# Low halves of the down projection's rest weights on VectorE, with two sums of product 6 moved behind them

## The chip, the cores and the metric

One core of a Trainium2 chip runs the whole program. The metric is the device time in microseconds. The kernel before takes 2112.26 us (median of 3 runs, 2108.97 to 2113.3). Engines are named as the profile names them: PE is TensorE's matmul and PEld its weight load, DVE is VectorE, ACT is ScalarE, POOL is GpSimd and SP is SyncE, which here only issues transfers. A line such as L361 is line 361 of the kernel before.

## The reference

Two layers of a decoder trunk on 512 tokens of width 1024, in float32. Each layer has a SwiGLU block, a mixer and a second SwiGLU block, each between two RMS norms:

```python
def swiglu(h, w_gate, w_up, w_down):
    return (jax.nn.silu(h @ w_gate) * (h @ w_up)) @ w_down

for l in range(DEPTH):                       # DEPTH = 2, D_MODEL = 1024, D_FF = 2816
    gn = norm_gains[l]
    h = rms_norm(x, gn[0])
    x = x + 0.5 * rms_norm(swiglu(h, w_ffn1_gate[l], w_ffn1_up[l], w_ffn1_down[l]), gn[1])
    ...
    x = x + rms_norm(mixed @ w_out[l], gn[3])
    h = rms_norm(x, gn[4])
    x = x + 0.5 * rms_norm(swiglu(h, w_ffn2_gate[l], w_ffn2_up[l], w_ffn2_down[l]), gn[5])
```

The change lies in the product with `w_down`, 2816 rows by 1024 columns, which runs four times: twice in each of two layers. Its result goes through a norm and is added to the residual x.

## The kernel before

**Precision.** Every float32 operand is split in two: a high half, rounded to the format that TensorE multiplies fast (`whi` for weights), and a low half, which is the operand less its high half (`wlo`). A product of two operands is three matmuls (`mm3`): high by high, high by low, low by high. In the down projection the activations are the stationary operand and the weights move, so the second of the three matmuls is the first one that reads `wlo`.

**The weight stream.** `ws` (class `Stream`) takes the weights in order through four raw buffers of 128x1024 (`w32`) and six pairs of split buffers (`whi`, `wlo`). An item is a raw weight or a combination of several. `ahead` splits items up to three ahead of the one in use, as long as fewer than six are in flight. A unit of kind "u" is split by a cast on ScalarE (L352) and a subtraction on VectorE (L361). A unit of kind "v" is split by the same cast, a multiplication by -1 on ScalarE that writes into the low half (L356), and a transfer issued by GpSimd that adds the raw weight to it (L359). When a raw buffer has been read, SP issues the load of a later weight into it.

**The down projection** (`down`, L698, with `fast` set in the four SwiGLU blocks). Its 22 blocks of 128 weight rows are treated in two ways. Blocks 0 to 15 with all columns and all tokens form a 2x2 matrix of quarters that is multiplied by seven products instead of eight (`quarters`, L927), in the order 1, 3, 7, 2, 6, 5 and, later, 4. Blocks 16 to 21 are the rest rows; they are multiplied directly, three units of two blocks for each half of the columns. The order on TensorE around the change is: product 6, product 5, the rest units' second column half for the token blocks 0 and 1, product 4, the same units for the token blocks 2 and 3, with transposes of the normed output between.

Each product has eight blocks in four pieces q = 0 to 3, one stream item each. A function of its own (`side1` to `side7`) is called before each piece, and brings the work that is to run beside it. The ones that matter here:

- `side6` splits activations for later products; at piece 3 it splits the first three of the six rest rows (`ready`, which casts on ScalarE at L430 and subtracts on VectorE at L431).
- `side5` splits the last three rest rows at piece 0. At piece 1 it issues the fetch (`fetch`): the output norm's gain and the eight tiles of the residual, 256 KB each, from memory (L737).
- `quarter` splits the pieces of the seven products (cast L285, subtraction L293) and forms the sums of weight quarters that later pieces need (L260).
- `add` (L943) sums product results into the output quarters on VectorE (L945). After product 6 come the sums into `c12` (from the first product's p1) and `u3`, after product 5 those into `c12` and `c22`. Each sum is two operations of 128x512, one for each token block.
- `half` (L830 to L833) adds the rest rows' result to the quarters' result, takes squares on ScalarE and multiplies by the gain. `post` (L851) adds it to the residual, `norm` (L862) prepares the next norm, and `turn` transposes the normed tokens for the next block on TensorE.

**Order.** TensorE's instructions run in the order of the text. Those of the other engines are ordered by the Tile framework's scheduler from the text's order and an estimate of times. `pin` ties an instruction behind the one that stands before it in the text on the same engine. `ws.hold` does so only while `ws.tight` is set, and casts of stream items are pinned while `ws.pinned` or `ws.tight` is set; `side6` sets `ws.pinned`. In the kernel before `ws.tight` is set only in the gate and up projections.

**Accumulators.** Five PSUM tiles are named `acc` and three `aux`. Products 6 and 5 write to two `acc` tiles each.

## Time and profile before

| | us |
|---|---|
| runs (3) | 2108.97, 2113.3, 2112.26 |
| median | 2112.26 |
| profiled execution, as timed | 2113.47 |
| its span on the profile | 2111.7 |
| mean granted clock of TensorE over the span | 0.989 |

The span runs from the program's first instruction to its last and is the basis of every view of the profile. Times in a timeline count from its start. A timeline row gives start and length, engine, line, operation, output and inputs by the program's names, the shape and how many like instructions are merged (x2), and in brackets the idle time of the engine just before, with what ended it. A row of waits gives who waited for whom, the microseconds in all, how many times, and the longest. Ends of matmuls are modelled: two in a row overlap on the page, so the pace of TensorE is read from their starts. A group row gives the count, the busy time in all and the mean of one in ns.

### The profile page before, as it was taken

How to read it: one execution, taken by the hardware profiler on the slowest of the kernel's cores; microseconds unless marked ns; L12 is line 12 of the kernel's file. 1: busy time of each engine (PE TensorE's matmuls, PEld its weight loads, DVE VectorE, ACT ScalarE, POOL GpSimd, SP SyncE). 2: the span in 40 equal slices, each digit the busy share in tenths (PEclk: the TensorE clock that was granted, in tenths of full speed). 3: DMA queues.
4: the chain of work that ended last, by engine and by line, in shares of the span. 5: the costliest groups of instructions: out<-in, count | busy, mean ns of one | idle time of the engine just before them, and what ended most of it. 6: DMA issues, size and time to landing. Idle time of an engine off the chain costs nothing. (4 is left out here: it accounts for less than half of the span.)

```text
span 2111.7 us, 36595 instructions
## 1 busy us (share of the span) xinstructions
PE 2083.1 (99%) x13561; PEld 1868.5 (88%) x13561; DVE 1621.3 (77%) x2897; ACT 1263.1 (60%) x2218; POOL 277.2 (13%) x330
## 2 busy tenths in 40 slices
PE   9999999999999999999999999999999999999997
PEld 7899987887888999998799998788778989999986
DVE  5887887766786787888788878967677758878886
ACT  6566686456454555658755666854654545666683
POOL 0011141000000011113101111400000000111140
PEclk9999999999999999999999999989999999999998
DMA  8677798312236368779858777973122553787794
GB/s 244 154 189 179 181 203 224 130 61 70 71 101 204 106 159 192 176 185 206 214 145 194 188 180 202 195 205 101 50 81 61 135 185 101 182 193 185 174 205 125
DMA packets 168531, 334.37 MB, mean 158 GB/s; under 512 B 19264, under 2 KB 85280, under 8 KB 168352
## 3 DMA queue, kind: packets, MB, share of 16 engines
q1 hardware_dynamic: 122416, 228.16, 32.4%
q0 software_dynamic: 45792, 103.83, 29.1%
q8 instruction: 106, 1.74, 0.3%
q14 instruction: 73, 0.60, 0.1%
q10 hardware_dynamic: 144, 0.05, 0.0%
HBM read 213.43 MB, written 14.73 MB: 108 GB/s over the span
## 5 line engine op out<-in xcount | busy, mean ns | idle before, releaser
L114 PE MATMUL acc<-s,whi 128*128 128x256 f32 (+1 forms) x4976 | 1051.3, 309 | 0.9 <-ACT whi L352 0.8
L114 PEld LDWEIGHTS acc<-s,whi 128*128 128x128 f32 x4976 | 808.8, 191 | 48.1 <-issue 3.2
L114 PE MATMUL acc<-s,wlo 128*128 128x256 f32 (+1 forms) x2488 | 764.8, 307 | 0.1
L114 PEld LDWEIGHTS acc<-s,wlo 128*128 128x128 f32 x2488 | 475.1, 191 | 23.1 <-DVE wlo L361 0.4
L114 PE MATMUL acc<-whi,s 128*128 128x512 f32 x1360 | 441.6, 393 | 0.0
L352 ACT CAST whi<-w 128x1024 fp32r<-128x1024 f32 (+1 forms) x309 | 287.0, 932 | 156.2 <-PE acc L114 89.8
L359 POOL DMA_DIRECT2D wlo<-w x190 | 163.6, 861 | 1292.1 <-DVE wlo L361 502.1
L352 ACT CAST whi<-tt 128x1024 fp32r<-128x1024 f32 x160 | 167.6, 1048 | 255.3 <-DVE tt L346 200.6
L114 PEld LDWEIGHTS acc<-whi,s 128*128 128x128 f32 x1360 | 255.3, 188 | 57.6 <-ACT whi L352 1.6
L361 DVE TENSOR_TENSOR wlo<-tt,whi 128x1024 fp32r<-128x1024 f32 x160 | 196.0, 1225 | 136.0 <-ACT whi L352 133.7
L114 PE MATMUL acc<-wlo,s 128*128 128x512 f32 x680 | 265.2, 390 | 0.2 <-DVE wlo L293 0.2
L114 PE MATMUL aux<-s,whi 128*128 128x256 f32 (+1 forms) x1296 | 239.2, 285 | 0.0
L361 DVE TENSOR_TENSOR wlo<-w,whi 128x1024 fp32r<-128x1024 f32 (+1 forms) x119 | 143.3, 1213 | 81.4 <-ACT whi L352 79.6
L114 PEld LDWEIGHTS aux<-s,whi 128*128 128x128 f32 x1296 | 202.7, 192 | 1.1 <-issue 0.5
L114 PE MATMUL aux<-s,wlo 128*128 128x256 f32 (+1 forms) x648 | 184.3, 284 | 0.0
L356 ACT ACTIVATE wlo<-w 128x1024 fp32r<-128x1024 f32 (+1 forms) x190 | 165.7, 873 | 0.0
L114 PE MATMUL aux<-whi,s 128*128 128x512 f32 x432 | 153.2, 414 | 0.0
L114 PEld LDWEIGHTS acc<-wlo,s 128*128 128x128 f32 x680 | 127.8, 188 | 25.6 <-DVE wlo L293 0.6
L442 POOL DMA_DIRECT2D s<-s x128 | 111.0, 958 | 220.6 <-ACT s L430 100.4
L114 PEld LDWEIGHTS aux<-s,wlo 128*128 128x128 f32 x648 | 124.4, 192 | 0.3
L293 DVE TENSOR_TENSOR wlo<-s,whi 128x512 fp32r<-128x512 f32 x160 | 102.6, 685 | 12.5 <-ACT whi L285 12.4
L114 PE MATMUL aux<-wlo,s 128*128 128x512 f32 x216 | 91.7, 425 | 19.5 <-DMA wlo<-w 19.5
(181 smaller groups left out, 2474.1 us busy)
## 6 DMA issues: line engine op xcount, KB each, us to landing
w<-wall SPq DMA_DIRECT2D x267, 512.0 KB, 4.2
wlo<-w POOLq DMA_DIRECT2D x110, 512.0 KB, 5.4
w<-wall SPq DMA_DIRECT2D x224, 128.0 KB, 3.6
wlo<-w POOLq DMA_DIRECT2D x80, 256.0 KB, 3.4
s<-wall SPq DMA_DIRECT2D x128, 128.0 KB, 3.9
s<-s POOLq DMA_DIRECT2D x64, 256.0 KB, 4.5
x_d<-s SPq DMA_DIRECT2D x48, 256.0 KB, 2.1
s<-x_d SPq DMA_DIRECT2D x48, 256.0 KB, 6.6
```

Source lines behind the costliest of these rows:

```text
L114: nc.tensor.matmul(o, lhsT, rhs, start=start, stop=stop)
L293: pin(nc.vector.tensor_tensor(it.lo[:, h[c]], w[c], it.hi[:, h[c]].bitcast(F32), op=ALU.subtract))
L352: i = nc.scalar.copy(it.hi[:, c], w[:, c])
L356: i = nc.scalar.mul(it.lo[:, c], w[:, c], -1.0)
L359: nc.gpsimd.dma_start(it.lo[:, c].bitcast(F32), w[:, c], accum_op=ALU.add)
L361: self.hold(nc.vector.tensor_tensor(it.lo[:, c], w[:, c], it.hi[:, c].bitcast(F32), op=ALU.subtract))
L442: nc.gpsimd.dma_start(lo.bitcast(F32), src, accum_op=ALU.add)
```

## The change

Three things change. The rest units of the second column half become kind "u". In `side5` the last three rest rows are split at piece 1 instead of piece 0, and `ws.tight` is set there; it stays set until product 5's last sum. And the sum of product 6 into `u3` is kept back (`late.then`) and made at piece 3 of product 5; `add` now goes through `ws.hold`, so while `ws.tight` is set the sums keep the place that the text gives them.

`ahead` comes to the first rest unit in piece 0 of product 5, to the second in piece 1, to the third in piece 2 and to product 4's first piece in piece 3. So the text's order on VectorE from there on is: first rest unit's low half, last three rest rows, second and third unit's low halves, the two sums into `u3`, product 4's first piece, the sums into `c12` and `c22`.

```diff
@@ rows
-            def unit(j, h, kind="u"):
+            def unit(j, h):
                 c = 2 * j * P
                 self.src[self.n] = ...
-                self.plain(1, kind)
+                self.plain(1)
...
             for j in lead:
-                unit(j, 1, "v" if fast else "u")
+                unit(j, 1)
@@ down
             def side5(q):
-                if q == 0:
+                if q == 1:
+                    ws.tight = True
                     ready(kt)
-                elif q == 1:
                     fetch()
+                elif q == 3:
+                    late.then()
@@ quarters
         def add(o, a, b):
             for t in range(2):
-                nc.vector.tensor_tensor(o[t], a[t], b[t], op=ALU.add)
+                ws.hold(nc.vector.tensor_tensor(o[t], a[t], b[t], op=ALU.add))
             return o
...
         c12 = add(p1, p, p1)
-        add(u3, p, u3)
+        late.then = lambda p=p: add(u3, p, u3)
         p = product(5, two(acc), True, side=side5)
         add(c12, p, c12)
         c22 = add(two(big), p, u3)
+        ws.tight = False
```

## The prediction

> **What bounds the kernel now.** I read the page first, then TensorE's own waits, then the stretch where they lie, engine by engine.

> ```profile
> span 2111.7 us, 36595 instructions
> ...
> PE 2083.1 (99%) x13561; PEld 1868.5 (88%) x13561; DVE 1621.3 (77%) x2897; ACT 1263.1 (60%) x2218; POOL 277.2 (13%) x330
> ```
> ```profile
> PE aux L114 <- DMA wlo<-w: 19.5, 12, 5.0
> ```

> The matmul stream is the kernel: PE is busy for all but 28.6 us. Of that idle time 19.5 us lie in twelve waits for the transfer that finishes a weight's low half (`wlo`). Twelve is three rest units in each of four down projections, so these are the instructions the change touches. The timeline of PE in the first of the four, and the windows of all four, show that the waits cost more than their own length:

> ```profile
> 322.81 0.39 PE L114 MATMUL aux<-whi,s 128*128 128x512 f32 x1
> 326.43 0.79 PE L114 MATMUL aux<-wlo,s 128*128 128x512 f32 x1 [3.23 <-DMA wlo<-w]
> ...
> 330.73 0.79 PE L114 MATMUL aux<-wlo,s 128*128 128x512 f32 x1 [1.37 <-DMA wlo<-w]
> ...
> 333.91 0.80 PE L114 MATMUL aux<-wlo,s 128*128 128x512 f32 x1 [0.26 <-DMA wlo<-w]
> ```
> ```profile
> 326.43:335.77 9.34, 7.71 (x16) 5.14 (x17) 2.10 (x4) 2.36 (x6) 0.00 (x0) 0.50 1.05 300
> ```
> ```profile
> 311.92:322.81 10.89, 10.89 (x49) 9.01 (x48) 10.89 (x19) 9.71 (x15) 2.73 (x4) 1.00 0.98 249
> 322.81:340.11 17.30, 12.44 (x37) 8.71 (x36) 9.48 (x17) 6.72 (x16) 0.86 (x1) 0.70 0.96 287
> 1019.43:1036.23 16.80, 12.68 (x37) 8.87 (x36) 9.47 (x17) 6.89 (x16) 0.86 (x1) 0.70 0.97 293
> 1366.38:1386.46 20.08, 13.77 (x37) 9.69 (x36) 10.16 (x18) 7.95 (x17) 1.15 (x2) 0.66 0.84 250
> 2065.79:2081.56 15.77, 11.60 (x37) 8.06 (x36) 9.52 (x18) 7.35 (x16) 0.86 (x1) 0.78 0.69 175
> 311.92:351.02 39.10, 34.24 (x134) 26.76 (x133) 27.92 (x54) 25.36 (x48) 4.45 (x6) 0.87 0.80 229
> ```

> A window's columns are its length, then busy time of PE, PEld, DVE, ACT and POOL, the granted clock, the share of DMA time and GB/s. The first of these six is product 5: 48 matmuls in 10.89 us, 0.2269 us each, at clock 1.00. The next four start at the first matmul of the rest units and end at the first one of product 4. Between them stand 36 matmuls (two token blocks, six rows, three products), 8.17 us at that pace. They take 17.30, 16.80, 20.08 and 15.77 us, so **the rest units lose 9.13 + 8.63 + 11.91 + 7.60 = 37.3 us**: 19.5 of waiting, and the rest because the clock stands at 0.50 once the first wait is over, for 9.34 us in the first projection.

> Why the low half is late:

> ```profile
> 316.73 1.05 ACT L352 CAST whi<-w 128x1024 fp32r<-128x1024 f32 x1 [1.08 <-issue]
> 317.69 1.05 ACT L356 ACTIVATE wlo<-w 128x1024 fp32r<-128x1024 f32 x1
> ...
> 320.85 1.06 ACT L352 CAST whi<-w 128x1024 fp32r<-128x1024 f32 x1
> ```
> ```profile
> 319.03 0.86 POOL L359 DMA_DIRECT2D wlo<-w  x1 [6.11 <-DMA w<-wall]
> ```
> ```profile
> s<-x_d SPq DMA_DIRECT2D x8, 256.0 KB, 8.3
> wlo<-w POOLq DMA_DIRECT2D x3, 512.0 KB, 9.6
> ```

> The first weight is cast at 316.73, its negative is made by 318.74, and the adding transfer is issued at 319.03. Between 318 and 327 these three transfers take 9.6 us (median) to land, among eight 256 KB reads of the residual (8.3 us). PE wants the first low half at 323.03 and gets it at 326.4.

> **The change, part by part.**

> *Low halves on VectorE.* Per projection three ScalarE multiplies, three POOL issues and three 512 KB transfers go; three 128x1024 subtractions on VectorE come.

> ```profile
> L361 DVE TENSOR_TENSOR wlo<-w,whi 128x1024 fp32r<-128x1024 f32 x117 | 142.1, 1222 | 81.4 <-ACT whi L352 79.6 <-DMA w<-wall 0.6 <-DMA grow<-rows_d 0.3
> ```

> That is 3 x 1.22 = 3.67 us more on VectorE and 3 x 1.05 us (row 317.69) less on ScalarE. VectorE is the engine to watch: in product 5 it is busy 10.89 us of 10.89. So I lay out its order as the program pins it. E is the moment after product 5's last weight piece is split, R the first matmul of the rest units.

> ```profile
> 319.44 1.28 DVE L945 TENSOR_TENSOR s<-acc,s 128x512 f32<-128x512 f32 x2
> 320.64 1.88 DVE L431 TENSOR_TENSOR s<-s,s 128x512 fp32r<-128x512 f32 x3
> ...
> 336.21 0.69 DVE L830 TENSOR_TENSOR s<-aux,s 128x512 f32<-128x512 f32 x1 [7.68 <-PE aux L114]
> ```
> ```profile
> 1015.82 1.28 DVE L945 TENSOR_TENSOR s<-acc,s 128x512 f32<-128x512 f32 x2
> ```
> ```profile
> 1363.59 1.28 DVE L945 TENSOR_TENSOR s<-acc,s 128x512 f32<-128x512 f32 x2
> ```
> ```profile
> 2062.25 1.27 DVE L945 TENSOR_TENSOR s<-acc,s 128x512 f32<-128x512 f32 x2
> ```

> These rows, the sums of product 6 that now move, start at E: 319.44, 1015.82, 1363.59, 2062.25. With R from the windows, R - E is 3.37, 3.61, 2.79 and 3.54 us. A 128x512 operation costs 0.60 in a row (319.44 to 320.64 for two). In the changed kernel the first subtraction stands at E (its cast, done at 317.8, comes before), so the first low half is there at E + 1.2; the last three rows' splits end at E + 3.0, the second low half at E + 4.2, the third at E + 5.4. The third cast, which started at 320.85 when it stood behind two multiplies, ends at 321.9 at the latest, before VectorE is ready for it at 323.6. PE needs the low halves at matmuls 1, 7 and 13: R + 0.23, R + 1.59, R + 2.95, which is E + 3.6, 4.96, 6.32 in the first projection and E + 3.0, 4.38, 5.74 in the third, the tightest. All three are in time, by 0.2 to 2 us. **The whole 37.3 us leave this stretch.**

> *The moved steps.* The last three rows' casts on ScalarE now stand behind the first weight's cast, which waits for its weight until 316.73; each has half its width, so some 0.5 us, and they end at about 319.4. VectorE takes them from E + 1.2 = 320.6, so its own work hides the move; without that cover it would cost the 1.6 us of the three casts. The nine transfers of the fetch stay in the same piece of product 5 on SP's queue. The loads of the next weights, which had waited for the adding transfers, can now go among them from E + 1.2 on; the residual they might push back is first read at L851, 17 us after E. The two sums of product 6 (1.2 us) go behind the third low half. They hold two accumulators until E + 6.6; with those of product 5 and one of y all five are taken, and the next is asked for after product 4, 19 us after R.

> *What is late next.* Behind the third low half VectorE has the two sums (to E + 6.6), product 4's first piece (two splits, two sums, to 9.0), four sums of product 5 (11.4), two products with the gain (12.6), one sum of the first token block (13.2), the second and third piece of product 4 (14.4, 15.6), then the chain that ends in the residual, L851, which starts at E + 17.6. The cover that hid all this before was the 7.68 us in which VectorE waited for PE (row 336.21), and it is gone: from the start of product 5 to the end of product 4 VectorE was busy 27.92 of 39.10 us and now has about 31.4 in 30.0. PE is at product 4 at R + 8.17 and needs its second piece at R + 11.12, which is E + 14.5 in the first projection (0.1 to spare) and E + 13.9 in the third (0.5 late). Further on I compare lags:

> ```profile
> 341.64 1.41 DVE L851 SCALAR_TENSOR_TENSOR s<-s,rt,s 128x512 f32<-128x512 f32 x2
> ...
> 350.50 0.89 DVE L862 TENSOR_SCALAR s<-s,rt 128x512 f32<-128x512 f32 x2
> ```
> ```profile
> 355.08 0.60 PE L124 MATMUL acc<-ident,s 128*128 128x128 f32 x4
> ```
> ```profile
> 2086.54 1.41 DVE L851 SCALAR_TENSOR_TENSOR s<-s,rt,s 128x512 f32<-128x512 f32 x2
> ```
> ```profile
> 2090.62 1.04 PE L124 MATMUL acc<-ident,s 128*128 128x128 f32 x8
> ```

> Before, L851 starts 1.5 us after product 4 does (341.64 against 340.11); afterwards E + 17.6 against E + 11.5, 6.1 after it: VectorE lags 4.5 us more. The transposes at 355.08 had 4.1 us to spare on their first operand (350.50 + 0.44), so they wait up to 0.4 us, and 0.6 more in the third projection, whose R - E is shorter. In the last, the transposes at 2090.62 had 3.4 us on theirs (2086.54 + 0.71): 1.0 late. I take 0.4, 0.3, 1.0 and 1.0, **about 3 us given back**. Bounds: nothing, if the pinned order lets the critical operations go first; 4 x 2.5 if every lag of 4.5 comes out 2 us longer.

> [...]

> **The sum.** 37.3 - 3 = 34.3 us off the profiled 2111.7. The profiled execution took 2113.47 in all, the runs 2108.97 to 2113.3 with median 2112.26, all within 0.2% of each other. From the median: **2078 us**. Its own range is 2074.5 (nothing given back) to 2084.

> **The rivals.**

> *A long wait stays in two projections.* For it: the third projection has 0.2 us to spare at the second low half, and PE already waited 0.20 there for product 5's last piece:

> ```profile
> 1363.73 0.50 PE L114 MATMUL acc<-wlo,s 128*128 128x512 f32 x1 [0.20 <-DVE wlo L293]
> ```

> [...] Price: two times about 9.3 back, 2097 us.

> *The half clock has another cause than the waits.* Then only the waiting goes: 19.5 - 3, so 2096 us. Against it: 1.00 stands right before and the four stretches alone are slow.

> *It does not do what it says.* The subtractions come out behind other work in VectorE's queue and the halves arrive when the transfers did: 2112 us. The pins speak against it.

> *VectorE becomes the bound, and it is slower.* One mechanism: the third low half is over 3 us late, for instance because its weight lands late. Everything pinned behind it, sums, product 4's pieces, norms, is then late by the same, and PE meets one short wait after another up to the transposes, which keep the clock at half as the waits at 330.73 and 333.91 did. From there to product 4's end are 5.2 + 10.9 = 16.1 us of work: 16.1 more, with 3 of waiting 19 a projection, against 9.3 now. In three projections of four that is 3 x 9.7 - 8.6 = 20 us slower, 2133. For it: 31.4 us of work in 30.0. Against it: it takes 4 us more than the layout has at the third low half.

> **Chances.** Forecast 0.68; long wait in two 0.13; half clock stays 0.05; no effect 0.04; VectorE bound 0.10. Faster by over 0.2% (4.2 us, about what this kernel's measurement can tell) holds the first three: 0.86; within it 0.03; slower 0.11. The range 2074 to 2098 takes in the forecast and the first two rivals but for their edges.

> **What would show it.** No wait of PE for `wlo<-w` in the aux matmuls and clock 1.00 between product 5 and product 4, 8.2 us long in each projection; VectorE's subtraction right after product 5's last split, and no 7.68 us idle before L830; new waits of PE under 1 us each at product 4's second or fourth piece or at the transposes. Wrong would be a wait over 3 us anywhere there, or a first subtraction that starts after R.

## Result and profile after

The changed kernel takes 2078.21 us (median of 5 runs, 2077.91 to 2081.02) against 2112.48 us before (5 runs, 2108.97 to 2116.1). The ratio is 0.984, with a 95% interval of 0.9825 to 0.9854: 34.3 us, 1.6%, faster. In what follows lines of the changed kernel are shifted by two or three: L947 is the old L945, L832 the old L830, L835 the old L833, L853 the old L851, L864 the old L862.

The page of the changed kernel, its span, busy times and granted clock by slice:

```profile
span 2076.3 us, 36563 instructions
...
PE 2067.7 (100%) x13561; PEld 1860.7 (90%) x13561; DVE 1632.1 (79%) x2909; ACT 1251.3 (60%) x2206; POOL 268.2 (13%) x318
...
PEclk9999999999999999999999999999999999999999
```

PE is idle for 8.6 us of the span instead of 28.6. VectorE has twelve more instructions, GpSimd and ScalarE twelve fewer each: three in each of four projections. Who PE still waits for, all rows of that view:

```profile
PE acc L124 <- DVE s L853: 3.1, 2, 2.6
PE aux L114 <- DVE eps_t L137: 1.1, 1, 1.1
PE acc L114 <- DVE s L531: 0.3, 1, 0.3
```

The twelve waits for `wlo<-w` are gone, with nothing in their place in the rest units. The windows of these units in the first two projections, from their first matmul to product 4's first:

```profile
323.04:331.20 8.16, 8.16 (x38) 6.76 (x36) 8.16 (x13) 3.99 (x10) 0.00 (x0) 1.00 1.03 392
1010.59:1018.81 8.22, 8.22 (x38) 6.81 (x37) 8.22 (x13) 4.16 (x10) 0.00 (x0) 1.00 1.01 374
```

They were 17.30 and 16.80 us at clock 0.70. The other two run from 1348.76 to 1356.92 and from 2036.59 to 2044.75, 8.16 us each. So the four gave up 9.14 + 8.58 + 11.92 + 7.61 = 37.3 us. VectorE's timeline in the first projection shows the layout:

```profile
319.46 1.22 DVE L361 TENSOR_TENSOR wlo<-w,whi 128x1024 fp32r<-128x1024 f32 x1
320.60 1.89 DVE L431 TENSOR_TENSOR s<-s,s 128x512 fp32r<-128x512 f32 x3
322.40 2.36 DVE L361 TENSOR_TENSOR wlo<-w,whi 128x1024 fp32r<-128x1024 f32 x2
324.67 1.29 DVE L947 TENSOR_TENSOR s<-acc,s 128x512 f32<-128x512 f32 x2
...
331.87 0.69 DVE L832 TENSOR_TENSOR s<-aux,s 128x512 f32<-128x512 f32 x1
...
336.88 1.41 DVE L853 SCALAR_TENSOR_TENSOR s<-s,rt,s 128x512 f32<-128x512 f32 x2
```

The first low half is made at 319.46, as soon as product 5's last piece is split, and the other two stand in a pair at 322.40, the third ready at 324.76. From product 5 to L853 no row has idle time in brackets any more: the 7.68 us before L832 are used up.

The rest of the account comes from laying the starts of all 13,561 matmuls of the two traces side by side. Each row gives by how much the changed kernel came out ahead (minus) or behind (plus) in a stretch:

| stretch | us |
|---|---|
| start-up of the program | +0.2 |
| rest units, four projections | -37.3 |
| projection 3, product 5's last piece no longer waited for | -0.5 |
| product 4's pieces, projections 1 to 4 | +0.07, +0.32, +0.35, +0.28 |
| last projection, transposes and what follows | +1.26 |
| sum, up to the last matmul | -35.3 (spans: 2076.3 - 2111.7 = -35.4) |

### The profile page after: what moved, and what is told of

Its sections match the earlier page's. It is cut to its first block, busy times and chain, and to the rows that moved or that the text cites. A ratio compares the mean times of both kernels' runs of the same rounds, so it can differ in the third digit from the quotient of the medians.

```text
span 2076.3 us, 36563 instructions
## 1 busy us (share of the span) xinstructions
PE 2067.7 (100%) x13561; PEld 1860.7 (90%) x13561; DVE 1632.1 (79%) x2909; ACT 1251.3 (60%) x2206; POOL 268.2 (13%) x318
## 4 chain that ended last, share of the span: by engine, by line
PE 95%; DVE 2%; DMA 1%; ACT 1%; issue 1%; SPq 0%; DVEq 0%; ACTq 0%
PE acc L114 72%; PE aux L114 21%; PE aux L124 2%; DMA w<-wall 1%; DVE wlo L293 1%; DVE s L260 1%; PE acc L124 0%; DMA s<-xin 0%; DMA s<-wall 0%; DVE s L947 0%; SPq L240 0%; DVE s L853 0%; SPq L243 0%; ACT s L440 0%; ACT s L530 0%
## 5 line engine op out<-in xcount | busy, mean ns | idle before, releaser
L114 PE MATMUL acc<-s,whi 128*128 128x256 f32 (+1 forms) x4976 | 1051.4, 309 | 0.3 <-DVE s L531 0.3
L114 PEld LDWEIGHTS acc<-s,whi 128*128 128x128 f32 x4976 | 808.8, 191 | 47.5 <-issue 3.2
L114 PE MATMUL acc<-s,wlo 128*128 128x256 f32 (+1 forms) x2488 | 764.8, 307 | 0.1
L114 PEld LDWEIGHTS acc<-s,wlo 128*128 128x128 f32 x2488 | 475.1, 191 | 23.1 <-DVE wlo L361 0.4
L114 PE MATMUL acc<-whi,s 128*128 128x512 f32 x1360 | 441.7, 393 | 0.0
L352 ACT CAST whi<-w 128x1024 fp32r<-128x1024 f32 (+1 forms) x309 | 287.0, 933 | 160.3 <-PE acc L114 93.7
L352 ACT CAST whi<-tt 128x1024 fp32r<-128x1024 f32 x160 | 167.7, 1048 | 256.1 <-DVE tt L346 199.8
L359 POOL DMA_DIRECT2D wlo<-w x178 | 154.3, 867 | 1258.6 <-DVE wlo L361 496.6
L114 PEld LDWEIGHTS acc<-whi,s 128*128 128x128 f32 x1360 | 255.3, 188 | 57.4 <-issue 1.6
L361 DVE TENSOR_TENSOR wlo<-tt,whi 128x1024 fp32r<-128x1024 f32 x160 | 196.1, 1225 | 137.2 <-ACT whi L352 133.7
L114 PE MATMUL acc<-wlo,s 128*128 128x512 f32 x680 | 265.5, 390 | 0.0
L114 PE MATMUL aux<-s,whi 128*128 128x256 f32 (+1 forms) x1296 | 239.2, 285 | 0.0
L361 DVE TENSOR_TENSOR wlo<-w,whi 128x1024 fp32r<-128x1024 f32 (+1 forms) x131 | 157.7, 1214 | 82.7 <-ACT whi L352 81.7
L114 PEld LDWEIGHTS aux<-s,whi 128*128 128x128 f32 x1296 | 202.7, 192 | 1.1 <-issue 0.5
L114 PE MATMUL aux<-s,wlo 128*128 128x256 f32 (+1 forms) x648 | 184.3, 284 | 0.0
L356 ACT ACTIVATE wlo<-w 128x1024 fp32r<-128x1024 f32 (+1 forms) x178 | 153.3, 861 | 0.1
L114 PEld LDWEIGHTS acc<-wlo,s 128*128 128x128 f32 x680 | 127.7, 188 | 26.5 <-DVE wlo L293 1.7
L114 PE MATMUL aux<-whi,s 128*128 128x512 f32 x432 | 143.6, 390 | 0.0
L114 PEld LDWEIGHTS aux<-s,wlo 128*128 128x128 f32 x648 | 124.4, 192 | 0.3
L293 DVE TENSOR_TENSOR wlo<-s,whi 128x512 fp32r<-128x512 f32 x160 | 102.8, 688 | 9.9 <-ACT whi L285 9.9
L430 ACT CAST s<-s 128x512 fp32r<-128x512 f32 (+1 forms) x140 | 70.6, 547 | 44.5 <-DVE s L489 41.0
## 6 DMA issues: line engine op xcount, KB each, us to landing
w<-wall SPq DMA_DIRECT2D x267, 512.0 KB, 4.1
wlo<-w POOLq DMA_DIRECT2D x98, 512.0 KB, 5.4
wlo<-w POOLq DMA_DIRECT2D x80, 256.0 KB, 3.4
s<-s POOLq DMA_DIRECT2D x64, 256.0 KB, 4.5
x_d<-s SPq DMA_DIRECT2D x48, 256.0 KB, 4.5
s<-x_d SPq DMA_DIRECT2D x48, 256.0 KB, 5.2
```

What stands on the lines that cost most here:

```text
L114: nc.tensor.matmul(o, lhsT, rhs, start=start, stop=stop)
L293: pin(nc.vector.tensor_tensor(it.lo[:, h[c]], w[c], it.hi[:, h[c]].bitcast(F32), op=ALU.subtract))
L352: i = nc.scalar.copy(it.hi[:, c], w[:, c])
L356: i = nc.scalar.mul(it.lo[:, c], w[:, c], -1.0)
L359: nc.gpsimd.dma_start(it.lo[:, c].bitcast(F32), w[:, c], accum_op=ALU.add)
L361: self.hold(nc.vector.tensor_tensor(it.lo[:, c], w[:, c], it.hi[:, c].bitcast(F32), op=ALU.subtract))
```

## Experiments

Each kernel was timed against runs of the kernel before on the same chip.

**The subtractions alone.** The kernel before with its order untouched and only the kind of the units changed:

```diff
-                unit(j, 1, "v" if fast else "u")
+                unit(j, 1)
```

> The kernel before with the rest units' low halves on VectorE, and nothing else: the last three rows and the sums of product 6 keep their old place ahead of the first subtraction. Theory (the late transfers were the loss; the order only trims what VectorE is late): the first low half ends at E + 1.2 + 1.8 + 1.2 = E + 4.2 and PE needs it at E + 3.6, 3.8, 3.0 and 3.8 in the four projections, so one wait of 0.4 to 1.2 us each, clock 1.00; 2 to 3 us more than the changed kernel: about 2080.5. Rival (without the new order VectorE is late enough to halve the clock): two or more projections lose some 9 us again, 2095 or more.

Measured: 2080.27 us (2079.89 to 2081.72), ratio 0.9846 (0.9831 to 0.986), span 2079.9. The waits in the rest units are now VectorE's own:

```profile
PE aux L114 <- DVE wlo L361: 3.1, 4, 1.1
```

So replacing the transfers gives all but about 2 us. What the order adds is visible as these four waits of 0.39 to 1.12 us; in the times alone it is near the limit of what they can tell.

**The order alone.** The changed kernel, with the low halves made by the transfers as before:

```diff
-                unit(j, 1)
+                unit(j, 1, "v" if fast else "u")
```

> The changed kernel's order and pins, with the low halves made as before, by ScalarE and an adding transfer. Theory (the transfers are the loss): PE still waits for them some 4 us or more in each projection and the clock falls to 0.50 behind it; 2108 to 2120. Rival (the order alone frees the path): 2080 to 2095.

Measured: 2108.84 us (2106.31 to 2112.04), ratio 0.998 (0.9971 to 0.999), span 2108.3.

```profile
PE aux L114 <- DMA wlo<-w: 19.8, 10, 3.9
```

The waits for the transfers are what they were before (19.5 us). The moved splits and sums do nothing about them. In the second projection, against the expectation, the clock did not fall behind its waits of 2.90, 0.81 and 1.35 us: it is 1.00 from 1021.21 to 1029.21. The time is still some 4 us under the kernel before. The mean granted clock of the two profiled executions is 0.994 here and 0.989 before, which goes the same way; whether the order or chance did that, no run shows.

**The sums of product 6 in their old place.** The changed kernel without the deferral:

```diff
-        late.then = lambda p=p: add(u3, p, u3)
+        add(u3, p, u3)
```

> The changed kernel with the two sums of product 6 back ahead of the rest units' low halves. Theory: every low half comes 1.2 us later than in the changed kernel, the second at E + 5.35 against a need of E + 4.4 to 5.2: waits of 0.2 to 1 us in each projection, clock 1.00, 1.5 to 2.5 us in all: about 2080. Rival (the moved sums carry the gain): over 2090.

Measured: 2079.49 us (2078.36 to 2080.34), ratio 0.9841 (0.9826 to 0.9855), span 2077.1. The two sums then stand before the second low half and PE waits 0.56 us in the first projection and 0.73 us in the second, 1.3 us in all; the other two show no wait, though one was expected in each. The span grows by 0.8 us. The direction is the expected one, but against the changed kernel's 2078.21 the times overlap.

**The residual's reads taken out of the transfers' way.** The kernel before, with the eight reads of the residual issued behind the loads of the next weights:

```diff
+            if not fast:
+                reads()
+        def reads():
...
-                    nc.sync.dma_start(xt[t][h], x_d[t, h])
+                    i = nc.sync.dma_start(xt[t][h], x_d[t, h])
+                    if fast:
+                        pin(i)
```

> The kernel before with the eight reads of the residual put behind the loads of the next weights on SP, so that the adding transfers have no such reads beside them. Theory (each transfer is late by crowding, and the clock falls only after a wait of some 3 us): the transfers land in about 5.4 us instead of 9.6, PE waits about 1.2 us at the first and 1 to 2 us at the second and third, and the clock stays at 1.00 where no wait is over 3 us; about 4 us a projection, 2090 to 2098 if the later reads hold up nothing else. Rival 1 (a transfer takes its 7 to 10 us without the reads too): no change, 2112. Rival 2 (any wait halves the clock): waits shorter, slow stretch as before, about 2103.

Measured: 2106.02 us (2103.54 to 2106.7), ratio 0.9964 (0.9951 to 0.9977), span 2101.8: a miss by 8 us or more. Ten waits of 18.5 us remain. The DMA issues with their median times to landing, first in the first projection (319 to 326 us), then in the last (2050 to 2060 us):

```profile
wlo<-w POOLq DMA_DIRECT2D x3, 512.0 KB, 5.3
w<-wall SPq DMA_DIRECT2D x1, 512.0 KB, 7.5
...
s<-x_d SPq DMA_DIRECT2D x8, 256.0 KB, 10.2
wlo<-w POOLq DMA_DIRECT2D x3, 512.0 KB, 9.8
```

The last projection has no weights left to load, so there the reads went out beside the transfers as before, and the transfers took 9.8 us; where the reads came later they took 5.3. So beside the reads the transfers took nearly twice as long here (in the kernel before, 9.6 us in the first projection). But without them the first transfer, issued at 320.16, still landed at 324.73, 4.6 us later and 1.7 us after PE asked for it, and the third, with the next weight's load beside it, took 7.9 us. PE's waits in the first projection:

```profile
324.77 0.50 PE L114 MATMUL aux<-wlo,s 128*128 128x512 f32 x1 [1.74 <-DMA wlo<-w]
327.59 0.51 PE L114 MATMUL aux<-wlo,s 128*128 128x512 f32 x1 [1.16 <-DMA wlo<-w]
332.10 0.50 PE L114 MATMUL aux<-wlo,s 128*128 128x512 f32 x1 [2.85 <-DMA wlo<-w]
```

PE asked for the first low half at 323.03, 2.9 us after the issue: the quickest of the three transfers took 4.6 us and could not meet that. Nor would 4.6 us have done from the issue in the kernel before, at 319.03, 4.0 us ahead. The three waits, 5.75 us in all, cost this projection little more than their length (6.6 us by the starts of the matmuls, against the changed kernel): the matmuls behind them take 0.50 us on the page, not the 0.79 of the kernel before, and the granted clock is 1.00 from 327.59 to 336.10. In the third projection it fell behind a wait of only 2.83 us (0.73 from 1364.18 to 1370.60). Both asked for the next set.

**A wait put back without any transfer.** The changed kernel, with n extra sums of 128x512 into an unused buffer (counted on at 0.60 us each) pinned on VectorE behind the first low half, so that the second and third come later. Nothing is left out of the computation.

```diff
                 if q == 1:
                     ws.tight = True
+                    idle = big()
+                    for _ in range(n):
+                        pin(nc.vector.tensor_tensor(idle, src[kt - 1], src[kt - 1], op=ALU.add))
                     ready(kt)
```

n = 4:

> The changed kernel with four extra 128x512 sums on VectorE (2.4 us, their result is not used) right behind the first rest unit's low half. The second low half is then about 1.4 us too late (it had about 1 us to spare). Theory (a short wait costs its own length, no clock with it): one wait of 1.2 to 2 us in each projection, clock 1.00; 6 to 10 us more than the changed kernel, 2084 to 2088. Rival (any wait halves the clock): 4.5 us more in each, 2102 or more. Rival (VectorE has slack all along): 2078 to 2080.

n = 6:

> The same with six extra sums (3.6 us; their result is not used): one wait of 2.5 to 3.2 us in each projection. Theory: just under or at the length after which the clock falls; 2089 to 2093 where it holds in all four, 4.5 us more for each projection where it falls, up to 2111. Rival (the low clock came with the transfers, not with the waiting): 2089 to 2093 and 1.00 in all four.

n = 8:

> The same with eight extra sums (4.8 us; their result is not used): one wait of 3.6 to 4.4 us in each projection. Theory (idle time halves the clock, whatever it waits for): clock 0.50 behind each wait for some us; 15 to 19 us of waiting and about 4.5 a projection for the clock, 2108 to 2116. Rival (the low clock came with the transfers): 1.00 behind the waits, 2093 to 2097.

n = 2, and n = 6 once more:

> Two extra sums of 0.60 us behind the first low half, so everything behind it is 1.2 us later. The four and the six extra sums left waits of 1.50 to 1.83 us for 2.4 us and 3.04 to 3.23 us for 3.6 us added, so 0.4 to 0.9 us of delay were hidden in each projection. If only what is not hidden counts, the waits here are 0.3 to 0.8 us each, with a few tenths behind them at product 4, the clock stays at 1.00 in all four stretches, and the time is 2080 to 2083 us. If short waits can cost the clock too, as the 1.82 us wait did with four sums, at least one stretch shows a clock under 0.8 and the time is 2083 to 2090 us.

> The kernel with six extra sums once more. In its first profile waits of 3.23, 3.04, 3.06 and 3.18 us left the clock at 1.00, 0.63, 1.00 and 0.63. If what decides lies in the program (which projection, what went before), the second and fourth projection are slow again and the span is within 1 us of 2097.9. If it lies in the moment, where a wait falls against something that runs on its own, other projections or another number of them are slow, and each one more or less moves the span by some 4 us.

| n | added as measured, four projections | median us (runs) | span over the changed kernel's | PE's waits for `wlo` in the rest units |
|---|---|---|---|---|
| 2 | 5.3 | 2086.59 (2086.52 to 2087.22) | +8.6 | 1.02, 0.23, 0.31, 0.46 |
| 4 | 11.1 | 2091.23 (2090.64 to 2091.79) | +12.6 | 1.83, 1.82, 1.71, 1.50 |
| 6 | 17.0 | 2100.15 (2098.53 to 2101.61) | +21.6 | 3.23, 3.04, 3.06, 3.18 |
| 6 | 17.0 | 2099.94 (2098.21 to 2103.21) | +20.1 | 3.12, 3.18, 3.37, 2.83 |
| 8 | 22.8 | 2108.46 (2105.43 to 2109.66) | +30.4 | 4.59, 4.27, 5.34, 4.76 |

The extra sums (L803) took longer than counted on: 0.67 us each with two and 0.71 us with eight, by VectorE's rows in the first projection for n = 2 and n = 8 (1.33 and 5.70 us from the first of them to the next operation). The second column of the table holds what they took.

```profile
322.30 1.42 DVE L803 TENSOR_TENSOR s<-s 128x512 f32<-128x512 f32 x2
323.63 1.89 DVE L431 TENSOR_TENSOR s<-s,s 128x512 fp32r<-128x512 f32 x3
```
```profile
320.57 5.78 DVE L803 TENSOR_TENSOR s<-s 128x512 f32<-128x512 f32 x8
326.27 1.89 DVE L431 TENSOR_TENSOR s<-s,s 128x512 fp32r<-128x512 f32 x3
```

The set teaches two things. First, the clock. With eight sums the waits come from VectorE alone, and the stretch behind the first wait runs at about half the clock:

```profile
329.34:335.44 6.10, 6.10 (x14) 4.84 (x15) 6.10 (x10) 0.00 (x0) 0.00 (x0) 0.51 0.60 197
335.44:339.00 3.56, 3.56 (x17) 2.96 (x16) 3.56 (x7) 0.72 (x2) 0.00 (x0) 1.00 0.32 117
```

So the half clock came here behind idle time of TensorE alone (4.59 us in this projection); no adding transfer serves these units any more. But the length of the wait alone doesn't decide. With six sums the first and third projections kept the full clock behind waits of 3.23 and 3.06 us, the second and fourth, with 3.04 and 3.18 us, did not:

```profile
328.05:332.05 4.00, 4.00 (x18) 3.31 (x19) 4.00 (x6) 0.04 (x1) 0.00 (x0) 1.00 0.97 342
1020.20:1024.20 4.00, 4.00 (x9) 3.14 (x10) 4.00 (x6) 0.00 (x0) 0.00 (x0) 0.50 0.97 329
...
1365.74:1369.74 4.00, 4.00 (x18) 3.31 (x19) 4.00 (x6) 0.26 (x1) 0.00 (x0) 1.00 0.95 328
2057.96:2061.96 4.00, 4.00 (x9) 3.14 (x10) 4.00 (x7) 0.00 (x0) 0.00 (x0) 0.50 0.01 4
```

In the last of these rows the DMA share is 0.01: the clock stood at 0.50 with next to no transfers under way. The same kernel profiled again slowed down in all four. So it lies in the moment, not in the program. Each pair of rows is the stretch behind the wait, and the one after it:

```profile
327.50:331.66 4.16, 4.16 (x11) 3.27 (x12) 4.16 (x7) 0.00 (x0) 0.00 (x0) 0.60 0.99 339
331.66:335.66 4.00, 4.00 (x19) 3.28 (x18) 4.00 (x7) 0.00 (x0) 0.00 (x0) 0.99 0.49 176
1020.46:1024.67 4.21, 4.21 (x11) 3.31 (x12) 4.21 (x7) 0.00 (x0) 0.00 (x0) 0.59 1.01 362
1024.67:1028.67 4.00, 4.00 (x19) 3.29 (x18) 4.00 (x8) 0.00 (x0) 0.00 (x0) 1.00 0.52 180
...
2057.71:2062.00 4.29, 4.29 (x12) 3.35 (x13) 4.29 (x7) 0.00 (x0) 0.00 (x0) 0.64 0.01 4
2062.00:2066.00 4.00, 4.00 (x18) 3.33 (x17) 4.00 (x8) 0.00 (x0) 0.00 (x0) 0.96 0.00 0
```

In which steps the clock changed is laid out further down, under the hardware.

Second, the price of the delay itself. Two sums add 5.3 us and the span grows by 8.6. Laid beside the changed kernel's matmuls, 3.2 us of these lie in the rest units and 2.2 at product 4's pieces: together about what was added. The other 3.2 us are no price of the delay. 1.0 lies at product 5's last piece in the first projection, ahead of the extra sums: in this execution ScalarE waited for a raw weight until 290.81, in the changed kernel's until 289.11. And 2.2 us are the same for every n from 2 to 8: 1.1 in the second layer's gate and up projections and 0.37 around the transposes of each of the first three down projections. In all these kernels the scheduler also gave VectorE and ScalarE a somewhat different order behind the rest units, which is the likely reason; no run separates the two. The clock stays full with n = 2 (0.999 over the span). Only about the first 1.0 us of a delay is hidden: in the changed kernel the second low half is ready that long before PE needs it (323.6 against 324.62 in the first projection).

## Why the prediction was right

The forecast of 2078.0 us meets 2078.21.

- **The loss in the rest units (37.3 us), and that all of it leaves.** Right, to 0.1 us in each projection. That only the transfers had to go for it is shown by the subtractions alone (2080.27) against the order alone (2108.84).
- **The layout on VectorE.** Right. First subtraction at E (319.46), second and third ready by about E + 4.1 and E + 5.3 (predicted 4.2 and 5.4), L853 at E + 17.4 (predicted 17.6). No low half was late. The margin was thin, as it said: with 1.3 us more in front, all four projections waited.
- **The third projection as the tightest.** Not borne out. Its 2.79 us between E and R were short because product 5's last piece was itself late on VectorE before; without that wait R - E is 1348.76 - 1345.21 = 3.55, no shorter than the others (3.58, 3.27 and 3.08).
- **The moved casts, reads and sums at no cost.** Right for what they cost; the sums' deferral is worth 0.8 us in the span, the whole order some 2 us.
- **About 3 us given back.** Right in kind, somewhat too large, and in part at other places: 0.07, 0.32, 0.35 and 1.54 us in the four projections, 2.3 in all, against 0.4, 0.3, 1.0 and 1.0. The predicted 1.0 for the last projection's transposes was near (1.26 with what follows). What the first three lost lies at product 4's fourth piece, at the matmul that first reads the low half VectorE splits for it. Their transposes were to be late because VectorE's lag of 4.5 us would last to the end of the chain. It didn't, as the end of that chain in the first projection shows, against the transposes that need it:

```profile
345.06 0.88 DVE L864 TENSOR_SCALAR s<-s,rt 128x512 f32<-128x512 f32 x2
```
```profile
346.24 0.60 PE L124 MATMUL acc<-ident,s 128*128 128x128 f32 x4
...
2054.92 1.32 PE L124 MATMUL acc<-ident,s 128*128 128x128 f32 x8 [0.47 <-DVE s L853]
```

L864 starts 13.86 us after product 4's first matmul (331.20), 10.39 before: VectorE had made up 1 us of the 4.5 by then, and the first operand is there 0.7 us early (345.06 + 0.44 against 346.24) instead of 0.4 late.

- **That the sum meets the median to 0.2 us** is luck. It forecast 34.3 us off the span, and the span came down by 35.4: 0.7 less was given back than 3, and 0.5 was won at product 5's last piece, a term that the sum does not hold. The medians came down by 34.3 because the profiled execution of the kernel before was 1.0 us above the median of its five runs. The bounds 2074.5 and 2084 were counted from the profiled span, the forecast from the median; from the median they are 2075 and 2085.
- **How long a wait the clock bears.** The run with the reads late took it to fall only behind some 3 us. Not borne out: it fell behind 1.82 us (n = 4, second projection: 0.72 over the 6.00 us behind it) and held behind 3.23 us (n = 6, first: 1.00 over the 4.00 us behind it). The forecast did not suffer, since no wait at all was left in the rest units.
- **Rivals.** No long wait stayed in any projection. That the half clock has another cause than the waits is refuted: with the transfers gone, waits of 4.27 to 5.34 us for VectorE brought it back in all four projections (n = 8: 0.50 to 0.54 behind them). VectorE did not become the bound, but the delays show how near it is: 2.8 us more in each projection (n = 4) give back 13 of the 34 us, 5.7 us more (n = 8) give back 30, part of it by the clock.

Of the expectations the price of the delays failed with two and four sums. With two, 2086.59 us at a full clock stands against 2080 to 2083 for that case; with four, 2091.23 against at most 2088, and one projection lost the clock. They took a sum for 0.60 us, and left out product 4's pieces and the 2.2 us that every one of these kernels loses behind the rest units. With six sums the time, 2100, fits two falls at 4.5 us each, but by luck: a fall cost some 2.7 us (6.1 and 6.2 us in the rest units of the second and fourth projections against 3.5 and 3.4 in the others), and the rest is the longer sums and the 2.2 us. The second execution had four falls instead of two, each half as long, and its span differs by 1.5 us only. Eight sums came out in their range in the same way, with longer waits than forecast and shorter slow stretches: 3.4 or 6.8 us, where the kernel before had 6.8 to 13.7.

## What to carry to other kernels

Making a low half by a copy and an adding transfer serves only while the time from issue to landing fits ahead of the consumer. Here PE asked 4.0 us after the issue, and the transfers beside the rest units took 4.6 to 9.8 us in the cases read above; the subtraction on a busy VectorE takes 1.22 us. And a wait on TensorE had two prices here, its length and what the clock did behind it: look at the granted clock of the windows behind a wait before counting what its removal is worth. The second price came behind a wait of 1.82 us in one of these runs, and not behind one of 3.23 us in another; the steps laid out next go with that.

## What the runs showed of the hardware

The first slow stretch before began inside the wait. Its three steps, with the one ahead of them and the one behind:

```profile
322.10:325.51 3.41, 1.10 (x5) 0.56 (x3) 3.41 (x7) 3.38 (x6) 0.86 (x1) 1.00 1.05 255
325.52:328.92 3.40, 2.49 (x6) 1.82 (x6) 3.01 (x6) 3.27 (x8) 0.00 (x0) 0.50 1.10 282
328.93:332.33 3.40, 2.03 (x5) 1.32 (x5) 0.00 (x0) 0.00 (x0) 0.00 (x0) 0.50 1.05 237
332.34:335.75 3.41, 3.15 (x8) 2.00 (x7) 0.00 (x0) 0.00 (x0) 0.00 (x0) 0.50 1.02 393
335.76:339.16 3.40, 3.40 (x16) 2.81 (x15) 2.95 (x5) 0.72 (x2) 0.00 (x0) 1.00 0.86 349
```

Steps of the same length with six sums: the first three rows are the first projection of the second execution, the fourth is a step of its last projection, the last two are the first projection of the first execution, laid off from the clock's return at about 1026.2 in its second projection (0.75 from 1024.20 to 1028.20), 205.0 steps behind 326.45:

```profile
324.93:328.33 3.40, 0.83 (x4) 0.70 (x5) 3.40 (x5) 2.22 (x6) 0.00 (x0) 1.00 1.01 377
328.35:331.75 3.40, 3.40 (x10) 2.63 (x9) 3.40 (x7) 0.00 (x0) 0.00 (x0) 0.50 0.98 327
331.76:335.16 3.40, 3.40 (x17) 2.77 (x15) 3.40 (x7) 0.00 (x0) 0.00 (x0) 1.00 0.54 192
...
2055.49:2058.89 3.40, 1.18 (x5) 1.01 (x6) 3.40 (x5) 1.61 (x4) 0.00 (x0) 1.00 0.08 31
```
```profile
323.04:326.45 3.41, 1.79 (x8) 1.13 (x7) 3.34 (x6) 3.38 (x9) 0.00 (x0) 1.00 0.97 357
326.46:329.87 3.41, 1.82 (x8) 1.52 (x9) 3.41 (x5) 1.64 (x4) 0.00 (x0) 1.00 1.00 362
```

A step with PE busy for 0.83 us is followed by one at half clock, and a busy one by the full clock again. The step at 2055.49, busy for 1.18 us, is followed by half clock as well, with next to no transfers under way (DMA share 0.08). Two steps that are busy for 1.8 us each leave the clock full. PE's idle time in these steps, and in those of the other three slow stretches before, read in the same way:

| clock in the step | PE idle in it, us | clock of the next step |
|---|---|---|
| full | before: 2.31, 2.01, 3.23, 3.03; six sums, second execution: 2.57, 2.22 | half |
| full | six sums, first execution: 1.62, 1.59 | full |
| half | before: 0.91, 1.37; 1.21, 0.56; 1.72, 0.73, 0.62; 0.60 | half |
| half | before: 0.26; 0.33; 0.00; 0.40; six sums, second execution: 0.00 | full |

These are readings of these executions: no run set the idle time within a step, and the ends of matmuls are modelled. They go with what the traces show side by side. The wait of 3.23 us that left the clock full (n = 6, first projection) lay across two steps, some 1.6 us in each. The wait of 1.82 us that halved it (n = 4, second projection) lay in one, by an estimate from the starts of the matmuls: they slow down at about 1017.5, and the wait is from 1015.07 to 1016.89. In the first slow stretch before, which holds the 9.34 us at half clock behind the first wait, the wait of 1.37 us lies in the second of the three steps, and the clock came back behind the third, with 0.26 us idle.

**An adding transfer of 512 KB between two on-chip buffers**, beside the rest units, took 4.6, 5.3 and 7.9 us from issue to landing (quickest, median and slowest of three) without the residual's reads in the first projection of the run with the reads late. Beside eight reads of 256 KB it took 9.8 us (median of three) in the last projection of that run and 9.6 us in the first of the kernel before.
